# Feed-forward down products as seven block products of eight, inner features in three parts

## The chip, the cores and the metric

The kernel runs on one core of one Trainium2 chip. The metric is the device time of one execution in microseconds (us); lower is better. An execution's span runs from its first to its last instruction, and the measured time holds a little more around it.

## The reference

Two transformer blocks follow each other, on 512 tokens of 1024 features, in float32. The first has two layers, each a token mixer, a cross attention and a gated feed-forward part. The second has one layer: three token mixers (one of them `s5`, a state space model), a cross attention and a feed-forward part with a convolution over three tokens. The inner width is 2816 in all three feed-forward parts. What the change touches is this:

```python
def swiglu(h, w_gate_up, w_down):
    g, u = jnp.split(h @ w_gate_up, 2, axis=-1)
    return (jax.nn.silu(g) * u) @ w_down

def conv_ffn(h, w_up, conv_w, conv_b, w_down):
    u = h @ w_up
    u = lax.conv_general_dilated(
        u, conv_w[:, None, :], window_strides=(1,), padding=[(CONV_W - 1, 0)],
        dimension_numbers=('NWC', 'WIO', 'NWC'), feature_group_count=2 * D_FF_2) + conv_b
    gate, val = jnp.split(u, 2, axis=-1)
    return (jax.nn.silu(gate) * val) @ w_down
...
x = x + swiglu(rms_norm(x, g_ffn[i]), w_gate_up[i], w_down[i])      # i = 0, 1
x = x + conv_ffn(rms_norm_2(x, norm_ffn[l]), ffn_w_up[l], ffn_conv[l], ffn_conv_b[l], ffn_w_down[l])
```

## The kernel before, in words

Features lie on the 128 partitions and the 512 tokens along the free axis. x is eight tiles of 128x512 that stay in SBUF. Every float32 operand is kept as two float32r parts, high and low, and a product of two operands is three matmuls (`Kit.mm3`, L274 to L282: high by high, high by low, low by high) into a PSUM bank of 128x512.

Weights come from DRAM in chunks of 128x512 or 128x384 (`Kit.load_split`, L306): SP issues the DMA into a raw tile (L308), ACT casts it to the high part (L310), and the engine that `Kit.by` names subtracts the high part from the raw tile for the low part (L312; VectorE in all three feed-forward parts). There are 7 raw tiles (NRAW) and 5 of each part (NW). `Kit.split` (L246 on ACT, L243 on DVE) does the same for activations.

`First.ffn` (L1166; called with i = 0 and i = 1) and `Second.ffn` (L2342) work in two halves of the inner features. In each half 11 up steps run, one for each inner tile: `proj_g` (L315) makes the gate tile and the value tile, 24 matmuls of 512 columns each. Then they are joined: L1178 (DVE, from PSUM), L1179 (ACT, silu), L1180 (POOL) and L1183 (DVE); or in the last stage the convolution, L2351 to L2354 (one DVE product from PSUM, one ACT step, two DVE steps that add a shifted product), L2365 (ACT) and L2368 (DVE). The result is split into high and low. After the 11 up steps come eight down steps, one for each output tile of 128 features: 11 inner tiles by three matmuls of 512 columns, the weights in chunks of 512, 512 and 384, and one addition of the bank to x (L671 or L1327 on DVE). After the second half, each x tile is at once normed (`normed`, `squares` L442 on ACT and L446 on POOL) or, at the end of the program, `last` takes its squares and `finish` scales and stores it.

During `First.ffn(1)` a job of the second block is woven in: `s5_make_g`, which computes the state space model's tables from its parameters (L1816 to L2034), mostly on DVE (operations of 128x16, 128x128 and 128x144) and POOL, with PE transposes at L2029 and L1994. `Kit.fill` after each up step runs as much of it as its argument says.

The order of instructions on each engine comes out of the tile framework's scheduler, which starts from the order in which the program emits them. Each engine works through its own list in order. Scratch tiles come from `Kit.room`, with a number of tiles for each tag.

## Time and profile before

| | before |
|---|---|
| median of 3 runs | 2791.21 us (2787.19 to 2793.16) |
| span of the profiled execution | 2782.0 us |
| feed-forward up stretch, last stage, second half | 119.7 us |
| feed-forward down stretch, last stage, first half | 60.4 us |
| feed-forward down stretch, last stage, second half | 60.6 us |
| up and down of `First.ffn(1)`, first half | 144.0 and 72.1 us |

The profile is of one execution of 2782.0 us from first to last instruction. The own time of that execution is not listed beside its span; the median of the three timed runs is 9.2 us above the span. In all rows PE is TensorE, DVE is VectorE, ACT is ScalarE, POOL is GpSimd and SP is SyncE; PEld is the weight load of a matmul, which runs beside the matmul before it. In a row of a group `out<-in` gives the names of the tiles, then their shapes, the number of instructions, the busy time, the mean of one in ns, and the idle time of the engine just before with what ended it.

### The profile page before, as it was taken

Reading aid. Unit: us, or ns where it says so; the run is one execution under the profiler, and the core shown is the slowest. Engines: PE = TensorE matmul, PEld = TensorE weight load, DVE = VectorE, ACT = ScalarE, POOL = GpSimd, SP = SyncE. Lnnn points to the kernel's source line nnn. Section 1 sums busy time; section 2 is a strip of 40 time slices with the busy share of each in tenths; the row PEclk is TensorE's granted clock in tenths of the full one; section 3 lists DMA queues with packets and bytes.
Section 4 is the critical chain, followed back from the end, with each engine's and each line's share of the span. In section 5 each row is a group of like instructions: output and inputs, shape, how many; then the busy total and the mean of one; then the engine's idle time right before and its main releaser. Section 6 shows DMA issues by size and latency. Waiting matters only on the chain.

```text
span 2782.0 us, 37160 instructions
## 1 busy us (share of the span) xinstructions
PE 2675.9 (96%) x13432; PEld 2152.4 (77%) x13432; DVE 1599.8 (58%) x3076; ACT 1186.2 (43%) x2208; POOL 517.4 (19%) x439
## 2 busy tenths in 40 slices
PE   8999999999999999899999889899999999999998
PEld 6668878888776787678887777687878788888886
DVE  4676654344357967973445567535443556675673
ACT  4566543233345765332334331425223445543442
POOL 5224121011211131250112331112131300100001
PEclk8999999999999999999999989699999999999999
DMA  4112223323322131333433344312211433233332
GB/s 151 35 42 77 72 84 93 101 95 95 110 78 74 49 103 56 109 121 114 142 96 131 113 163 116 99 61 62 81 54 61 124 117 102 83 96 95 99 95 68
DMA packets 172520, 258.51 MB, mean 93 GB/s; under 512 B 42528, under 2 KB 60832, under 8 KB 172320
## 3 DMA queue, kind: packets, MB, share of 16 engines
q1 hardware_dynamic: 172336, 256.13, 29.7%
q8 instruction: 106, 1.74, 0.3%
q14 instruction: 78, 0.64, 0.1%
HBM read 234.04 MB, written 22.15 MB: 92 GB/s over the span
## 4 chain that ended last, share of the span: by engine, by line
PE 54%; DVE 6%; issue 6%; POOL 2%; ACT 1%; DMA 0%; SPq 0%; POOLq 0%; DVEq 0%; ACTq 0%
PE ps_mm L280 14%; PE ps_mm L282 14%; PE ps_mm L281 14%; PE ps_ch L591 1%; DVE wl L312 1%; PE ps_si L2128 1%; POOL rs L466 1%; PE ps_tr L620 1%; PE ps_ch L1537 1%; PE ps_si L2124 0%; PE ps_si L607 0%; PE ps_ch L1610 0%; PE ps_ch L508 0%; PE ps_ch L1611 0%; PE ps_ch L1468 0%
## 5 line engine op out<-in xcount | busy, mean ns | idle before, releaser
L310 ACT CAST wh<-wraw 128x512 fp32r<-128x512 f32 (+1 forms) x777 | 474.5, 614 | 935.4 <-PE ps_mm L281 657.1
L312 DVE TENSOR_TENSOR wl<-wraw,wh 128x512 fp32r<-128x512 f32 (+1 forms) x691 | 484.3, 704 | 359.3 <-ACT wh L310 350.1
L280 PE MATMUL ps_mm<-xs,wh 128*128 128x512 f32 x1544 | 624.2, 404 | 6.2 <-ACT wh L310 5.7
L282 PE MATMUL ps_mm<-xs,wl 128*128 128x512 f32 x1544 | 612.8, 397 | 8.2 <-DVE wl L312 6.7
L281 PE MATMUL ps_mm<-xs,wh 128*128 128x512 f32 x1544 | 614.1, 398 | 0.5 <-DVE xs L262 0.3
L280 PEld LDWEIGHTS ps_mm<-xs,wh 128*128 128x128 f32 x1544 | 293.9, 190 | 77.0 <-issue 9.1
L282 PEld LDWEIGHTS ps_mm<-xs,wl 128*128 128x128 f32 x1544 | 293.7, 190 | 75.9 <-DVE wl L312 8.5
L281 PEld LDWEIGHTS ps_mm<-xs,wh 128*128 128x128 f32 x1544 | 293.8, 190 | 63.3 <-DVE xs L262 4.5
L446 POOL TENSOR_TENSOR acc<-acc,za 128x512 f32<-128x512 f32 x59 | 82.2, 1393 | 732.1 <-ACT za L442 730.4
L280 PE MATMUL ps_mm<-za,wh 128*128 128x512 f32 x460 | 183.5, 399 | 5.6 <-ACT za L246 5.0
L282 PE MATMUL ps_mm<-za,wl 128*128 128x512 f32 x460 | 182.7, 398 | 1.3 <-DVE wl L312 1.3
L281 PE MATMUL ps_mm<-za,wh 128*128 128x512 f32 x460 | 181.3, 394 | 0.1
L312 POOL TENSOR_TENSOR wl<-wraw,wh 128x512 fp32r<-128x512 f32 x86 | 113.4, 1327 | 345.5 <-ACT wh L310 283.8
L1180 POOL TENSOR_TENSOR za<-za,za 128x512 f32<-128x512 f32 x44 | 58.3, 1325 | 508.5 <-ACT za L1179 508.5
L280 PEld LDWEIGHTS ps_mm<-za,wh 128*128 128x128 f32 x460 | 87.9, 191 | 25.0 <-ACT za L246 6.2
L282 PEld LDWEIGHTS ps_mm<-za,wl 128*128 128x128 f32 x460 | 87.8, 191 | 22.0 <-DVE wl L312 1.8
L280 PE MATMUL ps_mm<-zb,wh 128*128 128x512 f32 (+1 forms) x284 | 100.3, 353 | 4.6 <-ACT zb L246 4.1
L281 PEld LDWEIGHTS ps_mm<-za,wh 128*128 128x128 f32 x460 | 87.7, 191 | 20.7 <-DVE za L243 1.0
L281 PE MATMUL ps_mm<-zb,wh 128*128 128x512 f32 (+1 forms) x284 | 98.6, 347 | 0.0
L243 DVE TENSOR_TENSOR za<-ps_tr,za 128x512 fp32r<-128x512 f32 (+3 forms) x152 | 84.3, 558 | 24.6 <-ACT za L246 23.5
L282 PE MATMUL ps_mm<-zb,wl 128*128 128x512 f32 (+1 forms) x284 | 98.3, 346 | 0.0
L466 POOL TENSOR_TENSOR rs<-sm,neghalf 128x4 f32<-128x4 f32 (+2 forms) x32 | 44.8, 1399 | 279.4 <-DVE sm L465 273.0
(592 smaller groups left out, 5013.3 us busy)
## 6 DMA issues: line engine op xcount, KB each, us to landing
wraw<-w_gu SPq DMA_DIRECT2D x176, 256.0 KB, 2.6
wraw<-w_dn SPq DMA_DIRECT2D x96, 256.0 KB, 2.6
wraw<-w_up SPq DMA_DIRECT2D x88, 256.0 KB, 2.6
wraw<-w_gate SPq DMA_DIRECT2D x48, 256.0 KB, 2.6
wraw<-w_dn SPq DMA_DIRECT2D x48, 192.0 KB, 2.3
dram<-za SPq DMA_DIRECT2D x26, 256.0 KB, 2.2
zc<-dram SPq DMA_DIRECT2D x26, 256.0 KB, 5.0
wraw<-w_cd SPq DMA_DIRECT2D x24, 256.0 KB, 2.6
```

What stands on the lines that cost most here:

```text
L243: self.nc.vector.tensor_tensor(lo, src, hi.bitcast(F32), op=ALU.subtract)
L280: mm(out, ah, bh, start=start, stop=False, **kw)
L281: mm(out, ah, bl, start=False, stop=False, **kw)
L282: mm(out, al, bh, start=False, stop=stop, **kw)
L310: self.nc.scalar.copy(hl[0], raw)
L312: eng.tensor_tensor(hl[1], raw, hl[0].bitcast(F32), op=ALU.subtract)
L446: self.nc.gpsimd.tensor_tensor(self.acc[0], self.acc[0], sq, op=ALU.add)
L466: self.nc.gpsimd.tensor_tensor(r, ms, self.neghalf[:, :n], op=ALU.pow)
L591: self.kit.nc.tensor.matmul(p, a[:, b * 128 : b * 128 + 128], c[:, k0:k1], start=i == 0, stop=i == len(self.qk) - 1)
L620: kit.nc.tensor.transpose(tr[:, i * 128 : i * 128 + 128], self.e[b][:, c : c + n], kit.ident)
L1180: nc.gpsimd.tensor_tensor(a, a, st["rb"], op=ALU.mult)
L1537: mm(p[:, i * 256 : i * 256 + 256], blk(st["ka"], e, 2 * g + i), st["ar"][2 * g + i][rows_], start=True, stop=True)
```

## The change

The down products of all three feed-forward parts are made in blocks of 2x2: two output tiles by two inner tiles by the two halves of 256 tokens, with seven block products in place of eight. One block product of n inner pairs is 3n matmuls of 256 columns. The left factors are the weight blocks a11, a12, a21, a22 and sums of them (s1 = a21 + a22, s2 = s1 - a11, a11 - a21, a12 - s2), the right factors are halves of inner tiles and differences of them (t1 to t4).

- The inner features are three parts of 4, 4 and 3 pairs of tiles (`PARTS`), where there were two halves of 11 tiles. The weights lie in DRAM in the order that this needs.
- `forms` makes the right factors for a pair of inner tiles: four subtractions of 128x256, on POOL (on DVE for the very last pair), then one split of 128x256 and three of 128x512, where the pair had two splits of 128x512. They fill seven tiles of a new tag m.
- `blocks` loads four raw weight chunks for a pair of output tiles and a part (128x512, or 128x384 in the part of three), makes four sums of them on POOL, and splits all seven: seven casts on ACT, seven subtractions on DVE.
- `seven` makes the seven products in three banks (x, y, z), of which it uses 256 columns; `seven_added` adds the bank to a half of an x tile after each product, on DVE.
- `ffn_parts` runs the up steps one beyond the end of each part, then the four pairs of output tiles. `Kit.fill` after an up step gets 3.0 for 1.5 (and stands in the last stage too).
- There are 8 raw tiles for 7, 6 of each weight part for 5, and the rooms have other sizes. The normed x or the last squares are taken for two x tiles together.

```diff
-NRAW = 7
-NW = 5
+NRAW = 8
+NW = 6
+L, R = slice(0, S // 2), slice(S // 2, S)
+PARTS = 4, 4, 3
...
+    def forms(self, f0, f1, tiles, eng=None):
...
+        sub = (eng or nc.gpsimd).tensor_tensor
+        ta, tb = self.f(), self.f()
+        sub(ta[:, L], f0[:, R], f0[:, L], op=ALU.subtract)
+        sub(ta[:, R], f1[:, R], f0[:, R], op=ALU.subtract)
+        sub(tb[:, L], f1[:, R], ta[:, L], op=ALU.subtract)
+        sub(tb[:, R], f1[:, L], tb[:, L], op=ALU.subtract)
+        one = next(tiles)
+        out = {"b11": (one[:, L], one[:, R])}
+        self.split(f0[:, L], *out["b11"])
+        for z, a, b in ((f1, "b21", "b22"), (ta, "t1", "t3"), (tb, "t2", "t4")):
+            hl = next(tiles), next(tiles)
+            self.split(z, *hl)
+            out[a], out[b] = ([y[:, h] for y in hl] for h in (L, R))
+        return out
...
+    def blocks(self, w):
...
+        for j in range(2):
+            for h in range(2):
+                z = raw[j, h] = self.t([128, CW], "wraw", NRAW)[:, : n * 128]
+                nc.sync.dma_start(z.rearrange("p (k m) -> p k m", m=128), w[j, :, h * n : h * n + n, :])
...
+        def sum_(x, y, op):
+            z = self.f(n * 128, tag="s")
+            nc.gpsimd.tensor_tensor(z, x, y, op=op)
+            return z
...
+        yield both(a11)
+        yield both(a12)
+        s1 = sum_(a21, a22, ALU.add)
+        s2 = sum_(s1, a11, ALU.subtract)
+        yield both(s2)
+        yield both(s1)
+        yield both(sum_(a11, a21, ALU.subtract))
+        yield both(sum_(a12, s2, ALU.subtract))
+        yield both(a22)
...
+    def seven(self, w, xf, take):
...
+        def product(p, form, start):
+            hl = next(a)
+            for k, x in enumerate(xf):
+                self.mm3(p, [z[:, k * 128 : k * 128 + 128] for z in hl], x[form], start and k == 0, k == len(xf) - 1, skip_group_check=True)
...
+        x = self.bank()[:, L]
+        product(x, "b11", True)
+        take("p1", x)
+        yield us
+        y = self.bank()[:, L]
+        product(y, "b21", True)
+        take("p2", y)
+        yield us
+        product(x, "t2", False)
+        take("u2", x)
...
+        z = self.bank()[:, L]
+        product(z, "t1", True)
+        take("p5", z)
...
+        product(x, "t3", False)
+        take("u3", x)
...
+        product(z, "b22", False)
+        take("p35", z)
...
+        product(x, "t4", False)
+        take("c21", x)
...
+    def seven_added(self, w, xf, first, second):
...
+        to = dict(p1=(first, L), p2=(first, L), u2=(first, R), p5=(second, R), u3=(second, R), p35=(first, R), c21=(second, L))
+        def take(step, p):
+            z, h = to[step]
+            self.nc.vector.tensor_tensor(z[:, h], p, z[:, h], op=ALU.add)
...
+    def ffn_parts(self, up, w_dn, x, left):
...
+        for at, n in parts:
+            end = min(at + 2 * n + 1, 2 * tiles)
+            while c < end:
+                self.run(up(c, mid(c == 2 * tiles - 1)))
+                self.fill(3.0)
+                c += 1
+            i = parts.index((at, n))
+            for m in range(DT // 2):
+                self.run(self.seven_added(w_dn[i][m], pairs[at // 2 : at // 2 + n], x[2 * m], x[2 * m + 1]))
+                if i == len(parts) - 1:
+                    left(2 * m)
+                    left(2 * m + 1)
...
-                kit.run(kit.proj_g(I["w_gu"][i, half * (FT // 2) + c], xs, gate))
-                kit.fill(1.5)
-            for m in range(DT):
-                kit.run(kit.proj_g(I["w_dn"][i, half, m], mid, lambda j, p: self.down(m, p, g if half else None)))
...
+        kit.ffn_parts(up, parts_of(I["w_dn"][i]), self.x, lambda m: self.left(m, g))
...
-    kit.room("aaaa", a=50)
+    kit.room("aaaa", a=24, m=28, s=6)
...
-    kit.room("abbb", a=31, b=50-31)
+    kit.room("abbb", a=8, m=28, s=5, b=17)
```

In all, PE gets 1188 rows more (three parts with 924 matmuls of 256 columns for 528 of 512). The comments are gone, so lines have other numbers: after the change L339 is a weight chunk's low part in the up steps, L270 any low part of `split` (of weight blocks `wl` and of the factors `zm`), L360 to L363 the four subtractions of `forms`, L391 a sum of weight blocks, L447 an addition to x, L1341, L1333 and L1344 are L1178, L1180 and L1183 of before, L2130 to L2136 are L1972 to L1978, and L2509 to L2524 are L2351 to L2368. Three places show how rows move.

DVE in the down steps of `First.ffn(0)`, before: three low parts of a chunk, then an addition to x.

```order
L671 TENSOR_TENSOR x_76<-ps_ch_4819,x_76 128x512
L312 TENSOR_TENSOR wl_4916<-wraw_4913,wh_4915 128x512
L312 TENSOR_TENSOR wl_4922<-wraw_4919,wh_4921 128x384
L312 TENSOR_TENSOR wl_4963<-wraw_4960,wh_4962 128x512
L671 TENSOR_TENSOR x_90<-ps_si_4872,x_90 128x512
```

The same place after the change.

```order
L270 TENSOR_TENSOR wl_4831<-wraw_4822,wh_4830 128x512
L447 TENSOR_TENSOR x_76<-ps_mm_4683,x_76 128x256
L270 TENSOR_TENSOR wl_4849<-wraw_4824,wh_4848 128x512
L447 TENSOR_TENSOR x_90<-ps_si_4748,x_90 128x256
L270 TENSOR_TENSOR wl_4870<-zs_4867,wh_4869 128x512
L447 TENSOR_TENSOR x_90<-ps_mm_4683,x_90 128x256
```

A low part and an addition now take turns; the low part is of a product six further on, of a raw block or of a sum `zs`. POOL had no row in the down steps.

POOL in the same down steps after the change: the four sums of each group of seven products, with work of a later inner tile and pair between.

```order
L391 TENSOR_TENSOR zs_4727<-wraw_4688,wraw_4690 128x512
L391 TENSOR_TENSOR zs_4729<-zs_4727,wraw_4684 128x512
L391 TENSOR_TENSOR zs_4766<-wraw_4684,wraw_4688 128x512
L391 TENSOR_TENSOR zs_4785<-wraw_4686,zs_4729 128x512
L360 TENSOR_TENSOR za_4583<-za_4462 128x256
L391 TENSOR_TENSOR zs_4865<-wraw_4826,wraw_4828 128x512
L1333 TENSOR_TENSOR za_4541<-za_4541,za_3919 128x512
L391 TENSOR_TENSOR zs_4867<-zs_4865,wraw_4822 128x512
L361 TENSOR_TENSOR za_4583<-za_4541,za_4462 128x256
```

What moved here is new work on an engine that had none in this place, with two inputs in SBUF in each row.

DVE in `First.ffn(1)`, the last block of the woven job before the change, beside the eleventh up step (L1183 joins it, L243 splits it).

```order
L1978 SCALAR_TENSOR_TENSOR zb_12116<-zb_12116,zb_12129 128x144
L1183 TENSOR_TENSOR za_12043<-ps_mm_12059,za_12043 128x512
L1974 TENSOR_TENSOR zb_12115<-zb_12115,zb_12117 128x144
L1972 TENSOR_TENSOR zb_12115<-zb_11375,zb_11226 128x144
L1973 TENSOR_TENSOR zb_12117<-zb_11375,zb_11226 128x144
L1978 SCALAR_TENSOR_TENSOR zb_12116<-zb_12116,zb_12136 128x144
L243 TENSOR_TENSOR za_12086<-za_12043,za_12085 128x512
```

The end of the same block after the change, beside the eighth up step.

```order
L2130 TENSOR_TENSOR zb_12658<-zb_12085,zb_11940 128x144
L2131 TENSOR_TENSOR zb_12660<-zb_12085,zb_11940 128x144
L1341 TENSOR_TENSOR za_12830<-ps_mm_12805,za_11577 128x512
L2132 TENSOR_TENSOR zb_12658<-zb_12658,zb_12660 128x144
L2136 SCALAR_TENSOR_TENSOR zb_12659<-zb_12659,zb_12665 128x144
L339 TENSOR_TENSOR wl_12984<-wraw_12981,wh_12983 128x512
L270 TENSOR_TENSOR wl_13042<-wraw_13033,wh_13041 128x512
L1344 TENSOR_TENSOR za_12830<-ps_mm_12846,za_12830 128x512
```

The whole job now lies ahead of the ninth up step. Before the gate row L1341 of this excerpt, 62 rows of the job stand in a line without a row of the feed-forward part between them; before the change the block's 64 rows were spread from the tenth up step into the first down steps.

## Rows read from the trace of the kernel before

**Rows 1.** The page: busy time of each engine, and the chain that ended last by engine.

```profile
PE 2675.9 (96%) x13432; PEld 2152.4 (77%) x13432; DVE 1599.8 (58%) x3076; ACT 1186.2 (43%) x2208; POOL 517.4 (19%) x439
...
PE 54%; DVE 6%; issue 6%; POOL 2%; ACT 1%; DMA 0%; SPq 0%; POOLq 0%; DVEq 0%; ACTq 0%
```

**Rows 2.** Busy time by stretch: us, engines' busy us (instructions), granted clock, DMA share, GB/s.

```profile
1094.90:1238.90 144.00, 128.79 (x582) 106.12 (x581) 119.73 (x410) 53.40 (x91) 52.10 (x72) 0.95 0.36 116
1238.90:1311.00 72.10, 68.28 (x318) 53.98 (x317) 32.80 (x70) 14.86 (x26) 13.22 (x16) 0.93 0.35 110
1434.10:1494.60 60.50, 60.50 (x267) 49.63 (x265) 27.26 (x40) 27.72 (x47) 17.39 (x12) 1.00 0.32 99
1168.80:1180.65 11.85, 0.43 (x2) 0.04 (x2) 11.74 (x27) 2.28 (x4) 8.88 (x14) 0.62 0.31 107
2526.00:2586.40 60.40, 60.40 (x266) 49.54 (x265) 23.22 (x36) 15.60 (x27) 0.00 (x0) 1.00 0.32 98
2586.40:2706.10 119.70, 119.70 (x530) 99.07 (x529) 87.98 (x128) 57.69 (x87) 0.00 (x0) 1.00 0.31 96
2706.10:2766.70 60.60, 60.60 (x267) 49.73 (x265) 20.55 (x32) 22.62 (x36) 7.80 (x6) 1.00 0.19 55
```

**Rows 3.** Groups by line in the last stage's first down stretch, 2526.0 to 2586.4 us.

```profile
L282 PEld LDWEIGHTS ps_mm<-za,wl 128*128 128x128 f32 x88 | 16.5, 188 | 3.9
L312 DVE TENSOR_TENSOR wl<-wraw,wh 128x512 fp32r<-128x512 f32 x17 | 11.7, 687 | 18.0 <-ACT wh L310 18.0
L310 ACT CAST wh<-wraw 128x512 fp32r<-128x512 f32 x18 | 11.2, 623 | 30.9 <-PE ps_mm L281 30.9
...
L312 DVE TENSOR_TENSOR wl<-wraw,wh 128x384 fp32r<-128x384 f32 x7 | 3.9, 559 | 10.7 <-ACT wh L310 10.7
```

**Rows 4.** Timeline of PE, 995.95 to 1003.99 us: start, duration, instruction.

```profile
995.95 0.28 PE L281 MATMUL ps_mm<-zb,wh 128*128 128x256 f32 x1
...
998.54 0.28 PE L282 MATMUL ps_mm<-zb,wl 128*128 128x256 f32 x1
...
998.89 0.28 PE L282 MATMUL ps_mm<-wh,zb 128*128 128x256 f32 x1
...
1003.99 0.28 PE L282 MATMUL ps_mm<-wh,zb 128*128 128x256 f32 x1
```

**Rows 5.** Timeline at 283 us and at 1120.7 us: POOL and DVE side by side.

```profile
283.00 1.77 POOL L446 TENSOR_TENSOR acc<-acc,za 128x512 f32<-128x512 f32 x1
283.53 0.68 DVE L671 TENSOR_TENSOR x<-ps_mm,x 128x512 f32<-128x512 f32 x1
...
284.13 1.19 DVE L312 TENSOR_TENSOR wl<-wraw,wh 128x512 fp32r<-128x512 f32 x1
...
1120.68 0.18 DVE L1872 TENSOR_TENSOR zb<-zb 128x16 f32<-128x16 f32 x1
1120.74 1.29 POOL L1180 TENSOR_TENSOR za<-za,za 128x512 f32<-128x512 f32 x1 [6.89 <-ACT za L1179]
...
1120.89 1.17 DVE L1874 TENSOR_TENSOR zb<-zb 128x16 f32<-128x16 f32 x1
```

**Rows 6.** Waits, 1094.9 to 1240 us: engine, line, waited for: us, times, longest.

```profile
PE ps_ch L2029 <- DVE zb L2022: 11.4, 1, 11.4
```

**Rows 7.** Timeline of DVE: the gates of the first and the ninth up tile.

```profile
1109.56 0.69 DVE L1178 TENSOR_TENSOR za<-ps_mm,za 128x512 f32<-128x512 f32 x1 [1.37 <-ACT za L501]
...
1210.98 0.69 DVE L1178 TENSOR_TENSOR za<-ps_mm,za 128x512 f32<-128x512 f32 x1 [0.34 <-PE ps_mm L282]
```

**Rows 8.** Groups by line of small operations: DVE 1100 to 1260, POOL 1094.9, DVE 880, DVE 2586.4.

```profile
L1972 DVE TENSOR_TENSOR zb<-zb,zb 128x144 f32<-128x144 f32 x16 | 6.2, 388 | 0.0
...
L1949 POOL TENSOR_TENSOR zb<-zb,zb 128x256 f32<-128x256 f32 x1 | 0.9, 885 | 0.0
...
L1083 DVE TENSOR_TENSOR zb<-ps_mm,zb 128x256 f32<-128x256 f32 x4 | 1.7, 421 | 0.3 <-PE ps_mm L282 0.3
...
L2354 DVE SCALAR_TENSOR_TENSOR za<-za,vecs,za 128x511 f32<-128x511 f32 x21 | 15.8, 751 | 6.1 <-ACT za L2352 6.1
```

More of the change, by code (lines that the diff above doesn't have):

```diff
@@ L51, in tiled, with halved, parted, parts_of @@
     return c.reshape(-1, n, *c.shape[1:])
+def halved(w):
+    t = w.reshape(w.shape[0] // 128, 128, -1)
+    return np.concatenate([t[0::2], t[1::2]]).reshape(w.shape)
+def parted(w):
+    out, at = [], 0
+    for n in PARTS:
+        out.append(tiled(halved(w[at * 256 : (at + n) * 256])).reshape(-1))
+        at += n
+    return np.concatenate(out)
+def parts_of(src):
+    out, at = [], 0
+    for n in PARTS:
+        size = D * n * 256
+        out.append(src[at : at + size].rearrange("(c j p k m) -> c j p k m", j=2, p=128, k=2 * n, m=128))
+        at += size
+    return out
 def col(v):
@@ L327, in proj_late @@
+    def seven_added(self, w, xf, first, second):
[3 more added lines that the diff above has]
+            self.nc.vector.tensor_tensor(z[:, h], p, z[:, h], op=ALU.add)
+        return self.seven(w, xf, take)
     def proj_late(self, groups, last):
@@ L423, in flush, with mid, f @@
             self.fill(1.0)
+    def ffn_parts(self, up, w_dn, x, left):
+        parts, tiles, mids = [], sum(PARTS), []
+        for n in PARTS:
+            parts.append((2 * sum(PARTS[: len(parts)]), n))
+        pairs = []
+        held = (self.f(S, F32R, tag="m") for _ in range(7 * tiles))
+        def mid(last):
+            def f(z):
+                mids.append(z)
+                if len(mids) % 2 == 0:
+                    pairs.append(self.forms(*mids[-2:], held, self.nc.vector if last else None))
+            return f
+        c = 0
+        for at, n in parts:
[10 more added lines that the diff above has]
+                    left(2 * m + 1)
     def normed(self, m, x, g, squares=True):
@@ L1157, in cross, with left, ffn @@
                       lambda: kit.ended(O, 3))
-    def down(self, m, p, g):
+    def left(self, m, g):
         if callable(g):
-            self.add(m, p)
             g(m)
         else:
-            self.add(m, p, g)
-    def ffn(self, i, g=None):
+            self.kit.normed(m, self.x[m], g[:, m : m + 1])
+    def ffn(self, i, g):
         kit, nc, I = self.kit, self.nc, self.I
@@ L2355, in conv, with up, emit @@
             return a
[L2357 to L2380 removed]
+        def up(c, mid):
+            def emit(j, p):
+                if "rb" not in st:
+                    st["rb"] = kit.spread(kit.rstd(), 4)
+                a = conv(p, j * FT + c)
+                if j == 0:
+                    nc.scalar.activation(a, a, AF.Silu)
+                    st["a"] = a
+                else:
+                    nc.vector.tensor_tensor(a, a, st["a"], op=ALU.mult)
+                    mid(a)
+            return kit.proj_g(I["w_up2"][c], xs, emit)
+        for m in range(DT):
+            if self.x[m] is None:
+                raise ValueError(m)
+        kit.ffn_parts(up, parts_of(I["w_dn2"]), self.x, self.last)
     def last(self, m):
@@ L2468, in program @@
     s.cross()
-    kit.room("aaaa", a=50)
+    kit.room("aaaa", a=24, m=28, s=6)
     s.ffn()
```

90 lines of the change are left out of this document (42 added, 48 removed).

## The prediction

> **What bounds the kernel now.** I read the page first. PE is busy 96% of the span, VectorE (DVE) 58%, ScalarE (ACT) 43% and POOL 19%, and on the chain that ended last PE has 54% and DVE 6% [rows 1]. So a down stretch should be as long as its matmuls. The stretches show that it is: in the last stage's first down stretch PE is busy 60.40 of 60.40 us at granted clock 1.00 (2.4 GHz), DVE 23.22 us, POOL not at all; the second is 60.6 us [rows 2]. The two halves, 121.0 us, hold 528 matmuls of 512 columns, .229 us each. Their weight parts are made far ahead: ACT's casts wait for PE to give tiles back (30.9 us of idle) and DVE's low parts for ACT (18.0 us) [rows 3]. Fewer columns on PE are worth their time here, as long as DVE and POOL can take what replaces them.
>
> The first half of the second feed-forward part is different. There the woven job keeps DVE busy 119.73 of 144.00 us, PE stands at 128.79, and the granted clock is 0.95; the down stretch behind it takes 72.10 us [rows 2]. The undisturbed pair is 119.7 and 60.4 [rows 2], so 36 us go to the job. One wait, of transposes for DVE, is 11.4 us [rows 6], and in that stretch the clock falls to 0.62, between 1.2 and 2.4 GHz, after PE stood with 0.43 us of work in 11.85 [rows 2].
>
> **The change, part by part.**
>
> *Fewer columns.* The trace has no down product of 256 columns, but the same form elsewhere, each matmul with its own weight load: 22 starts from 995.95 to 998.54, .1177 us each, with a scratch tile moving and a weight chunk standing as after the change; and 45 from 998.89 to 1003.99, .1133 us, with the roles exchanged [rows 4]. I take .1177, whose operands are those of the change. 924 x .1177 = 108.8 us per part against 121.0: **-12.2**. The other end, .1133, gives 104.7: -16.3.
>
> *The seven splits and additions of a group.* A group of seven products is 84 matmuls (n = 4; 9.89 us) or 63 (n = 3; 7.42 us); there are eight of the first and four of the second. ACT's seven casts, .623 us each [rows 3], make 4.4 us: hidden. DVE has seven low parts at .687 and seven additions of 128x256 from PSUM at .421 [rows 3, 8]: 7.8 us, below 9.89 (n = 3, with .559 for .687: 6.9 below 7.42). New are POOL's four sums, 1.29 us each, and here a price hides. While POOL works on two SBUF tiles, a DVE operation whose inputs are both in SBUF is held: a 128x16 operation took 1.17 us where its neighbour took 0.18, and a low part 1.19 where .687 is usual [rows 3, 5]. An addition from PSUM beside the same POOL operation took 0.68, unharmed [rows 5]. POOL's row began at 1120.74 and the held one, short itself, ended at 1122.06, so a sum holds the port some 1.15 us. Sums and low parts then need 4 x 1.15 + 7 x .687 = 9.4 us of 9.89; with n = 3 and three quarters of 1.15, 3.45 + 3.91 = 7.4 of 7.42. It just fits if the additions lie beside the sums. Order gives them turns [low part, addition], so part of each sum will meet a low part. I add 0.1 us a group, **+1.2** per part. The bounds are nothing, and all the additions left over, 2.95 us in each group (below).
>
> The Trainium skill ("SBUF — State Buffer", section "SBUF: two separate sides") calls the pair of ports that DVE and GpSimd share an exclusive lock: whichever starts first has it for its whole instruction and the other fully blocks, and for DVE this concerns instructions with two SBUF inputs. The trace agrees in kind, with a hold of about 1.15 of POOL's 1.29 us; by the rule's whole 1.29 the sum of a group is 4 x 1.29 + 7 x .687 = 10.0 us, an estimate, which would make the group DVE's by 0.1 us.
>
> *The up steps.* `forms` adds 1.5 low parts a pair, 1.04 us of DVE, and four POOL subtractions at .885 [rows 8] or less. In the last stage DVE is busy 87.98 of 119.70 us and POOL idle [rows 2]: 11 x 1.04 us over 22 up steps fit. The cover is the rest of DVE, some 30 us. Cost: nothing. The steps run in parts of 9, 8 and 5, so that PE has an up step while a pair's factors are made; not for the last pair. There the factors wait for subtractions and splits after the last up tile, on DVE: some 3 x .421 + 3 x .687 = 3.3 us, against the two or so us that the scheduler covers with products of the earlier pairs. **+1** in the two parts of the first block. In the last stage the convolution's chain stands ahead, with two steps at .751 [rows 8] and the casts between: **+2.3**.
>
> *Ends.* Two x tiles, not one, are normed together: +.5, and +.8 at the end of the program, where their squares come before the last sum. SP issues four weight loads a group for six; DMA is at .19 to .36 [rows 2]: nothing. Other rooms and two more buffers move rows elsewhere; between -5 and +5, and I take -1.
>
> *The job.* It is now done by the ninth up step. Up to that gate the rows after the change, each at the mean of its line between 1090 and 1440 us in the trace, make 118.7 us of DVE where the same sum over the order before is 104.6; the trace took 101.4 for that stretch, 1109.56 to 1210.98 [rows 7], and scaled by that the new order takes 115.1. So the ninth gate comes 13.7 us later, in two places: ahead of the first transposes (factors of three pairs are in front of them), and in the last block, 64 rows at up to .388 [rows 8] with PE idle. Behind it nothing of the job is left, and of the 36 us above those that came after 1210.98 vanish: from there to the end of the part's last down stretch, 1494.6 [rows 2], it was 283.6 us; a clean run of 13.5 up steps at 10.88 and 121.0 us is 267.9, so 15.7. The balance is -2. The clock may take some back after a long wait, so I take **+2**, with -5 and +12 as ends.
>
> *The sum.* First part: -12.2 + 1.2 + 1 + .5 = -9.5. Last part: -12.2 + 1.2 + 2.3 + .8 = -7.9. Second part: -12.2 + 1.2 + 1 + .5 + 2 = -7.5. With -1 elsewhere: -25.9. The profiled execution spans 2782.0 us, so 2756.1; the median of the runs lies 9.2 above the span, so **2765** on the clock of the runs (2791.21 - 25.9). Its own range, 2757 to 2778, comes from half of the ends above.
>
> **The rivals.**
>
> *Fully fed.* The additions fall beside the sums, nothing is late, and a matmul takes between .1133 and .1177. For it: DVE is busy a third of the down stretch now [rows 2]. Against: the fit above has 0.5 us to spare. Three parts at -12.2 to -16.3, ends as above or none: 2742 to 2757, say 2750.
>
> *The shared port bounds the down steps* (the other side). A low part and an addition alternate in DVE's queue, so a held low part also holds the addition behind it, PE's next product on that bank waits, and ACT's next cast waits for PE. What part of the 2.95 us of additions isn't covered decides: half of it makes groups of 9.4 + 1.5 = 10.9 and 7.4 + 1.5 = 8.9, 122.8 us a part, slower than 121.0; the break-even is a little less than half. With +1.8 a part and +7 for the ends and the job: 2791.2 + 5.4 + 7 = 2804. All of it: 8 x 12.35 + 4 x 10.35 = 140 us, 2855. For it: the rows at 284 and 1120 us. Against: the addition from PSUM passes [rows 5].
>
> *The job eats its part's gain.* DVE is saturated in nine up steps, waits grow past 12 us, and the clock stays at 1.2 GHz for longer. Second part: -12.2 + 2.7 + 17 = +7.5 with the other two as summed: 2780.
>
> *Half the columns don't halve the time.* If the weight load bound it, at .188 each [rows 3], 924 would take 174 us and the three parts +158: 2950. The 67 matmuls of rows 4 speak against it.
>
> **How the numbers follow.** My forecast has .46, fully fed .26, the job .13, the port .13, the weight load .02. The range reaches from the lower end of fully fed, 2742, to 2798, which takes in the job's case and leaves out most of the port's. A measurement of this kernel tells 0.2% (5.6 us) from no change. Faster by more than that: the first three, less their upper tails, .80; within it: .07; slower: the port but its low end, and the weight load, .13.
>
> **What would show it.** In the changed profile's down stretches of the last stage: PE's matmuls .1177 apart, a part's three stretches together near 110 us, POOL at 4 to 5 us a group. Right on the port if low parts of the down steps average some .8 to 1.0 us while additions stay at .42. Wrong if PE waits there for low parts or additions by over a microsecond a group, if the wait for the job's first transposes is over 20 us, or if the last pair's factors cost over 4 us.

## The result, and the profile after

The changed kernel takes 2830.48 us (median of 4 runs, 2824.72 to 2831.86) against 2792.18 before (4 runs). The ratio is 1.0139, 95% interval [1.0121, 1.0156]: 1.4% slower, where I had forecast 0.9% faster. The profiled execution spans 2827.8 us, 45.8 more than before.

The page first; its columns are those of [rows 1].

```profile
PE 2674.0 (95%) x14620; PEld 2197.1 (78%) x14620; DVE 1892.4 (67%) x3466; ACT 1266.2 (45%) x2384; POOL 839.9 (30%) x703
...
PE 51%; DVE 10%; issue 4%; POOL 2%; ACT 2%; DMA 0%; POOLq 0%; DVEq 0%; SPq 0%; ACTq 0%
```

DVE is busy 293 us longer and POOL 323 (a row that is held counts as busy while it is held); DVE's part of the chain that ended last rose from 6 to 10%. The next view is busy time by stretch of the changed kernel (columns as in [rows 2]): the three feed-forward parts whole; then the three down stretches of `First.ffn(0)`; the first nine up steps of `First.ffn(1)` and its three down stretches; the three down stretches of the last stage.

```profile
366.10:737.10 371.00, 359.80 (x2005) 313.36 (x2004) 247.35 (x364) 152.54 (x261) 150.52 (x122) 0.99 0.31 94
1103.70:1531.20 427.50, 387.28 (x2161) 327.55 (x2162) 332.69 (x721) 167.54 (x293) 202.18 (x197) 0.95 0.35 105
2435.00:2812.40 377.40, 359.75 (x2001) 315.25 (x1999) 316.90 (x457) 179.06 (x295) 117.80 (x96) 0.98 0.28 84
...
471.40:512.50 41.10, 40.15 (x337) 39.75 (x337) 35.53 (x57) 17.71 (x29) 13.39 (x11) 1.00 0.34 99
599.60:641.40 41.80, 40.17 (x337) 39.81 (x336) 36.22 (x57) 17.70 (x29) 13.20 (x11) 1.00 0.33 98
695.80:737.10 41.30, 33.96 (x258) 31.18 (x258) 38.96 (x66) 23.01 (x44) 17.96 (x15) 1.00 0.28 85
1103.70:1261.10 157.40, 131.67 (x612) 99.62 (x613) 142.22 (x437) 53.77 (x95) 85.86 (x107) 0.88 0.33 103
1261.10:1304.30 43.20, 40.27 (x338) 39.86 (x337) 37.43 (x60) 17.32 (x30) 19.11 (x13) 1.00 0.57 175
1391.30:1432.70 41.40, 39.36 (x338) 38.80 (x338) 36.96 (x57) 17.71 (x29) 14.61 (x12) 1.00 0.35 104
1487.10:1531.20 44.10, 34.58 (x254) 32.14 (x253) 42.19 (x66) 27.01 (x52) 24.59 (x19) 0.96 0.26 79
2535.90:2583.00 47.10, 42.18 (x338) 41.76 (x338) 42.34 (x66) 21.20 (x35) 15.15 (x12) 0.93 0.32 92
2670.10:2716.90 46.80, 41.65 (x337) 41.24 (x336) 42.42 (x65) 21.17 (x35) 14.69 (x11) 0.96 0.30 91
2771.30:2812.40 41.10, 34.11 (x253) 31.86 (x252) 35.61 (x65) 21.75 (x42) 16.30 (x14) 0.96 0.07 20
```

Before, the three parts took 368.3, 399.7 and 363.6 us (from the run of matmuls that begins the first up step to the last matmul of the down steps), so they changed by +2.7, +27.8 and +13.8 us. The rest, +1.5, lies in stages that the change hardly touches. Of down stretches, four pairs should be 336 matmuls x .1177 = 39.5 us and three 29.7. None is: PE is busy in 34.0 to 42.2 us of stretches of 41.1 to 47.1, and DVE in 36 to 42 of each of the nine. (In the third line of `First.ffn(0)`'s stretches, .9 us of the 41.3 are four matmuls of the next stage.)

The matmuls are as forecast. Timeline of PE in the changed kernel: 51 starts, .1178 us each.

```profile
2551.09 0.28 PE L309 MATMUL ps_mm<-zm,wl 128*128 128x256 f32 x1
...
2557.10 0.28 PE L309 MATMUL ps_mm<-zm,wl 128*128 128x256 f32 x1
```

DVE is not. Groups by line on DVE in the first down stretch of `First.ffn(0)`, columns as in [rows 3].

```profile
L270 DVE TENSOR_TENSOR wl<-zs,wh 128x512 fp32r<-128x512 f32 x13 | 12.3, 949 | 0.8 <-ACT wh L273 0.5
L270 DVE TENSOR_TENSOR wl<-wraw,wh 128x512 fp32r<-128x512 f32 x10 | 9.5, 946 | 0.2
L447 DVE TENSOR_TENSOR x<-ps_mm,x 128x256 f32<-128x256 f32 x15 | 6.3, 418 | 1.4 <-PE ps_mm L309 1.1
```

A low part takes .95 us on average where it took .687 before [rows 3], and an addition from PSUM keeps its .42 [rows 8]. The timeline of POOL and DVE shows why.

```profile
2550.24 1.30 POOL L391 TENSOR_TENSOR zs<-wraw,wraw 128x512 f32<-128x512 f32 x1 [5.45 <-DVE wl L270]
...
2550.35 0.42 DVE L447 TENSOR_TENSOR x<-ps_mm,x 128x256 f32<-128x256 f32 x1 [0.19 <-PE ps_mm L309]
...
2552.22 1.30 POOL L391 TENSOR_TENSOR zs<-wraw,zs 128x512 f32<-128x512 f32 x1 [0.68 <-POOL zs L391]
...
2552.34 1.72 DVE L270 TENSOR_TENSOR wl<-zs,wh 128x512 fp32r<-128x512 f32 x1
```

The addition at 2550.35 runs beside the sum; the low part at 2552.34 waits for it, 1.72 us for a work of .687. In the last stage this happens at the start of the stretch too, where the convolution of the up step that runs ahead is on DVE; its shifted products have two SBUF inputs. Timeline of DVE and POOL there:

```profile
2538.47 2.40 DVE L2512 SCALAR_TENSOR_TENSOR za<-za,vecs,za 128x511 f32<-128x511 f32 x2
2538.63 1.70 POOL L391 TENSOR_TENSOR zs<-wraw,zs 128x512 f32<-128x512 f32 x1 [1.23 <-DVE wl L270]
...
2543.30 0.41 DVE L447 TENSOR_TENSOR x<-ps_mm,x 128x256 f32<-128x256 f32 x1
```

The two convolution steps take 2.40 us where 2 x .751 [rows 8] is 1.5; the row at 2543.30 is the first addition of the stretch. Waits of the changed kernel, 2535.9 to 2583.0 us, then 1103.7 to 1261.1 us (columns as in [rows 6]).

```profile
PE ps_mm L307 <- DVE x L447: 4.8, 1, 4.8
```

```profile
PE ps_ch L2187 <- DVE zb L2180: 17.4, 3, 9.1
PE ps_mm L307 <- DVE za L1341: 3.2, 1, 3.2
```

PE waits 4.8 us for the first addition, which stands behind held operations in DVE's list: seven held rows of DVE between 2526.5 us and the addition (low parts, splits and convolution steps) took some 4.9 us more than such rows take unheld, .68 or .75 us for each operation (an estimate from that timeline). Most of the rest of the stretch's excess of 7.6 us is a lower clock behind the wait: PE was busy 42.18 us with what is 39.5 at 2.4 GHz, and from 2541 to 2546 us the granted clock was 0.55, between 1.2 and 2.4 GHz. The job's transposes wait 17.4 us, in three pieces, where before they had 11.4 [rows 6].

### The profile page after: what moved, and what is told of

It reads as the page before. It is cut to its first block, busy times and chain, and to the rows that moved or that the text cites. A ratio compares the mean times of both kernels' runs of the same rounds, so it can differ in the third digit from the quotient of the medians.

```text
span 2827.8 us, 40698 instructions
## 1 busy us (share of the span) xinstructions
PE 2674.0 (95%) x14620; PEld 2197.1 (78%) x14620; DVE 1892.4 (67%) x3466; ACT 1266.2 (45%) x2384; POOL 839.9 (30%) x703
## 4 chain that ended last, share of the span: by engine, by line
PE 51%; DVE 10%; issue 4%; POOL 2%; ACT 2%; DMA 0%; POOLq 0%; DVEq 0%; SPq 0%; ACTq 0%
PE ps_mm L307 13%; PE ps_mm L308 13%; PE ps_mm L309 13%; PE ps_ch L746 1%; DVE wl L270 1%; DVE wl L339 1%; DVE za L2512 1%; PE ps_si L2286 1%; POOL rs L621 1%; PE ps_tr L775 1%; PE ps_ch L613 1%; PE ps_ch L1695 1%; PE ps_ch L1626 0%; DVE x L447 0%; PE ps_ch L1768 0%
## 5 line engine op out<-in xcount | busy, mean ns | idle before, releaser
L307 PE MATMUL ps_mm<-xs,wh 128*128 128x512 f32 (+1 forms) x1536 | 626.1, 408 | 10.6 <-ACT wh L337 5.8
L308 PE MATMUL ps_mm<-xs,wh 128*128 128x512 f32 (+1 forms) x1536 | 616.2, 401 | 5.3 <-DVE xs L289 5.0
L309 PE MATMUL ps_mm<-xs,wl 128*128 128x512 f32 (+1 forms) x1536 | 614.5, 400 | 2.1 <-POOL wl L339 1.5
L339 DVE TENSOR_TENSOR wl<-wraw,wh 128x512 fp32r<-128x512 f32 x547 | 402.3, 739 | 169.8 <-ACT wh L337 164.3
L307 PEld LDWEIGHTS ps_mm<-xs,wh 128*128 128x128 f32 (+1 forms) x1536 | 294.7, 192 | 84.1 <-issue 14.8
L308 PEld LDWEIGHTS ps_mm<-xs,wh 128*128 128x128 f32 (+1 forms) x1536 | 295.2, 192 | 70.7 <-DVE xs L289 10.4
L309 PEld LDWEIGHTS ps_mm<-xs,wl 128*128 128x128 f32 (+1 forms) x1536 | 294.8, 192 | 68.7 <-issue 3.3
L307 PE MATMUL ps_mm<-zm,wh 128*128 128x256 f32 x724 | 207.9, 288 | 29.8 <-DVE x L447 24.0
L308 PE MATMUL ps_mm<-zm,wh 128*128 128x256 f32 x724 | 205.6, 284 | 2.4 <-DVE zm L270 2.4
L339 POOL TENSOR_TENSOR wl<-wraw,wh 128x512 fp32r<-128x512 f32 x86 | 113.3, 1326 | 313.7 <-ACT wh L337 282.7
L309 PE MATMUL ps_mm<-zm,wl 128*128 128x256 f32 x724 | 205.1, 284 | 0.9 <-DVE wl L270 0.9
L307 PEld LDWEIGHTS ps_mm<-zm,wh 128*128 128x128 f32 x724 | 138.6, 192 | 35.8 <-DVE x L447 11.0
L308 PEld LDWEIGHTS ps_mm<-zm,wh 128*128 128x128 f32 x724 | 139.2, 192 | 3.7 <-DVE zm L270 3.4
L270 DVE TENSOR_TENSOR wl<-zs,wh 128x512 fp32r<-128x512 f32 (+1 forms) x144 | 134.2, 937 | 10.8 <-ACT wh L273 8.1
L309 PEld LDWEIGHTS ps_mm<-zm,wl 128*128 128x128 f32 x724 | 139.2, 192 | 1.1 <-DVE wl L270 1.1
L270 DVE TENSOR_TENSOR zm<-za,zm 128x512 fp32r<-128x512 f32 (+1 forms) x132 | 113.9, 863 | 38.2 <-ACT zm L273 32.9
L391 POOL TENSOR_TENSOR zs<-wraw,wraw 128x512 f32<-128x512 f32 (+1 forms) x72 | 93.5, 1298 | 138.1 <-DVE wl L270 70.6
L1333 POOL TENSOR_TENSOR za<-za,za 128x512 f32<-128x512 f32 x44 | 58.8, 1337 | 228.7 <-ACT za L1332 228.5
```

Source lines behind the costliest of these rows:

```text
L270: self.nc.vector.tensor_tensor(lo, src, hi.bitcast(F32), op=ALU.subtract)
L307: mm(out, ah, bh, start=start, stop=False, **kw)
L308: mm(out, ah, bl, start=False, stop=False, **kw)
L309: mm(out, al, bh, start=False, stop=stop, **kw)
L339: eng.tensor_tensor(hl[1], raw, hl[0].bitcast(F32), op=ALU.subtract)
L391: nc.gpsimd.tensor_tensor(z, x, y, op=op)
```

## The experiments

Theory A is that the shared port makes the loss: POOL's operations and DVE's with two SBUF inputs exclude each other. Theory B is that DVE simply has too much to do. C to G concern single places.

**The sums elsewhere, and gone.**

```diff
 # e1
-            nc.gpsimd.tensor_tensor(z, x, y, op=op)
+            nc.vector.tensor_tensor(z, x, y, op=op)
 # e2
-            z = self.f(n * 128, tag="s")
-            nc.gpsimd.tensor_tensor(z, x, y, op=op)
-            return z
+            return x
```

> The changed kernel (2830.5 us) with the four sums of weight blocks of each group on DVE in place of POOL. Theory A, the shared port: the low parts of the down steps last 0.82 to 0.95 us because POOL's sums hold them, so without POOL in the way they fall to 0.69, the four-pair down stretches of First.ffn(0) go from 41.1 and 41.8 us to 39.5 to 40.5, and the whole to 2810 to 2825 us. Theory B, DVE's load alone: four operations of 0.69 more in each group lengthen DVE's list from 7.8 to 10.5 us against 9.9 of PE, down stretches grow by 2 to 4 us each and the whole goes to 2840 to 2860 us.

> The changed kernel with the sums of weight blocks left out (the split takes the first operand of each sum as it is, so the products are of other weights); all else is as in the changed kernel. Theory A, the shared port: low parts at 0.69 us, four-pair down stretches at 39.5 to 40, the three-pair ones at 33 to 35 for 36 to 44, the whole 15 to 25 us below the changed kernel. Theory B, DVE's load alone: low parts keep 0.69 once POOL is out, but PE goes on waiting for additions, less than 8 us in all.

e1 took 2821.1 us, ratio 1.0102 [1.0060, 1.0143] to the kernel before. That interval overlaps the changed kernel's, so the stretches decide. DVE has more work and the stretch is shorter: 40.2 us in the first down stretch of `First.ffn(0)` for 41.1, and low parts are at .689, as theory A said. (The nine up steps of `First.ffn(1)` are not shorter, 160.6 us for 157.4.) Groups by line on DVE there, in e1:

```profile
L270 DVE TENSOR_TENSOR wl<-zs,wh 128x512 fp32r<-128x512 f32 x13 | 9.0, 689 | 0.7
L270 DVE TENSOR_TENSOR wl<-wraw,wh 128x512 fp32r<-128x512 f32 x10 | 6.9, 687 | 0.7 <-ACT wh L273 0.2
```

Theory B's lengthening did not come in `First.ffn(0)`. e2, which leaves the sums out, took 2789.8 us in a single execution, 40 below the changed kernel, more than either theory said. Stretches of e2: the first four-pair one, the last one of `First.ffn(0)`, and the first nine up steps of `First.ffn(1)`.

```profile
468.30:507.90 39.60, 39.60 (x338) 39.60 (x337) 31.72 (x57) 17.71 (x29) 1.12 (x1) 1.00 0.37 122
689.00:726.40 37.40, 33.71 (x258) 31.12 (x257) 34.61 (x66) 22.67 (x44) 10.50 (x7) 1.00 0.35 105
1093.30:1247.20 153.90, 130.78 (x611) 98.61 (x612) 136.46 (x437) 53.51 (x95) 79.17 (x102) 0.89 0.31 103
```

Without sums the first four-pair stretch is PE's 39.6 (40.3 in the last stage). The last stretch keeps 7.7 us above 29.7 and the job's stretch hardly moves, so the sums are not what makes these two long.

**The factors on DVE, alone and with the sums.**

```diff
 # e6, e12 (with e1's edit)
-        sub = (eng or nc.gpsimd).tensor_tensor
+        sub = nc.vector.tensor_tensor
```

> The changed kernel (2830.5 us) with the four subtractions of every pair's factors on DVE, as for the last pair, in place of POOL. Theory A, the shared port: on POOL they take up to 1.1 us each (40 rows, 43.6 us in First.ffn(1)) and hold the low parts and the job's operations, on DVE 0.42 each; the first nine up steps of First.ffn(1) go from 157.4 to 145 to 152 us and the whole falls by 5 to 15 us. Rival: they lie in slack or DVE has none, and the whole stays within 4 us.

> The changed kernel with both the sums of weight blocks and the subtractions of the factors on DVE, so that the change brings no work to POOL. Theory A, the shared port: no low part of the down steps is held any more, and what the two single moves gave (9 and 12 us, one of them from one look) adds up in part: 2808 to 2818 us. Theory B, DVE's load: DVE is then over 95% busy in every down stretch and the whole stays at 2818 us or above, far from the 2790 us that the kernel without the sums took.

> The kernel of e12 again, for its profile. Theory A: low parts and factors' splits at 0.69 us throughout, POOL with nothing but the gates, norms and the job in the feed-forward parts; against the changed kernel the first nine up steps of First.ffn(1) fall from 157.4 to 140 to 148 us, and the down stretches of the last stage from 47.0, 46.8 and 40.4 to 42 to 44, 42 to 44 and 36 to 38. Theory B: DVE is busy over 95% in every down stretch and First.ffn(0) gains nothing over the run with the sums on DVE.

e6 took 2818.5 us in a single execution, a fall of the size forecast but not in the place: the nine up steps stayed at 158.1 us. The stage of the mixers between the second and the last part, which has no edit, was 895 us there against 904; that is most of the 12. Its first down stretch of `First.ffn(0)` says more. Busy time of that stretch in e6, and a low part of its DVE:

```profile
466.10:505.60 39.50, 39.00 (x338) 38.81 (x337) 35.24 (x57) 17.71 (x29) 10.19 (x8) 1.00 0.32 102
...
L270 DVE TENSOR_TENSOR wl<-zs,wh 128x512 fp32r<-128x512 f32 x13 | 12.2, 940 | 1.2 <-ACT wh L273 0.9
```

The sums are on POOL and hold the low parts, .94 us on average, as in the changed kernel, and yet the stretch is 39.5 us. So four sums a group do fit there (the second stretch is 40.6); what does not fit is the sums together with what else POOL does beside them.

e12 took 2795.0 us, ratio 1.0025 [1.0007, 1.0043], better than theory A's 2808 to 2818 and far from B's: the same operations on DVE in place of POOL take back 35 of the 38 us. Stretches of e12b (the same kernel, a single execution of 2801.3 us): parts; then the first four-pair stretch and the last stretch of `First.ffn(0)`; the nine up steps and the last stretch of `First.ffn(1)`; the three stretches of the last stage.

```profile
363.60:726.00 362.40, 357.36 (x2001) 312.33 (x2000) 254.05 (x451) 153.06 (x260) 45.45 (x34) 0.99 0.31 95
1095.50:1517.30 421.80, 388.57 (x2163) 329.46 (x2164) 332.38 (x810) 166.75 (x292) 99.32 (x109) 0.95 0.34 107
2425.90:2784.20 358.30, 354.31 (x2001) 310.96 (x1999) 307.45 (x545) 181.07 (x294) 8.82 (x7) 1.00 0.29 89
...
469.00:508.60 39.60, 39.60 (x338) 39.59 (x337) 34.60 (x64) 17.70 (x29) 0.00 (x0) 1.00 0.35 103
689.70:726.00 36.30, 32.54 (x254) 30.52 (x253) 35.34 (x72) 22.01 (x43) 8.84 (x7) 1.00 0.26 84
1095.50:1245.80 150.30, 127.64 (x611) 96.36 (x612) 134.76 (x455) 50.90 (x90) 64.35 (x85) 0.90 0.32 106
1470.60:1517.30 46.70, 38.67 (x256) 36.20 (x255) 42.39 (x75) 26.38 (x51) 15.58 (x10) 0.85 0.24 74
2526.90:2566.40 39.50, 39.50 (x337) 39.50 (x336) 36.50 (x70) 18.94 (x31) 0.00 (x0) 1.00 0.35 103
2653.50:2693.10 39.60, 39.60 (x337) 39.57 (x336) 36.60 (x70) 19.04 (x31) 0.00 (x0) 1.00 0.33 101
2747.60:2784.20 36.60, 33.19 (x253) 31.46 (x251) 32.55 (x69) 21.05 (x40) 6.57 (x5) 0.95 0.08 22
```

With POOL out of it, DVE is busy 34.6 to 36.6 us of these four-pair stretches, and PE is never late: 39.5 us, the 336 matmuls and nothing else. The same DVE with less work of its own had cost 1.6 to 7.6 us a stretch when POOL worked beside it. (In `First.ffn(1)` the second four-pair stretch is 39.5 us too; the first, right behind the job, is 43.4.) Against the changed kernel the three parts gain 8.6, 5.7 and 19.1 us. Against its expectation the last stage did better (39.5 and 39.6 us for 42 to 44) and the nine up steps worse (150.3 for 140 to 148).

In the last stage neither move alone did that (its first stretch is 43.6 us in e1, 46.5 in e6). In e6 POOL's sums still hold the convolution's steps, up to 1.75 us for .75, and PE waits 4.0 us for the first addition. In e1 POOL's three subtractions just ahead of the stretch hold a sum and a split (1.11 and 1.23 us for .68), which is some 1.0 of the 2.3 us that PE waits; whether the order of DVE's list makes the rest is open.

The excess of the last stretches, 36.3, 46.7 and 36.6 us for 29.7, stays, and the middle one is longer than in the changed kernel (44.1). In the first block DVE is busy 35.3 of 36.3 and 42.4 of 46.7 us there, so theory B's load is the likely limit. In the last stage it is busy 32.6 of 36.6, less than in a four-pair stretch that had no late matmul; there PE's longest wait is 2.2 us, for the last pair's factors.

**The order of the parts and the step ahead.**

```diff
 # e4
-            end = min(at + 2 * n + 1, 2 * tiles)
+            end = min(at + 2 * n, 2 * tiles)
 # e7
-PARTS = 4, 4, 3
+PARTS = 3, 4, 4
```

> The changed kernel without the one up step past the end of each of the first two parts. Theory E: in the last stage that step's convolution chain stands on DVE ahead of the first products' low parts and additions and costs the waits of 4.8 and 4.6 us at the start of the down stretches (and some 2 us of lower clock behind each); without it the waits go, but the last pair's factors then come late, 3 to 6 us a stretch, so the whole is within 6 us of the changed kernel. Rival: the step is a plain loss, and the whole falls by 10 us or more.

> The changed kernel with the part of three pairs first and parts of four behind (3, 4, 4 for 4, 4, 3). Theory F: the last down stretches (36.3, 44.0 and 40.4 us where 252 matmuls at 0.1177 make 29.7) are long because the norm's or the last squares' work on DVE and POOL, which before had 60.5 us of down steps to lie beside, now has four groups of 7.4 us; beside groups of 9.9 us the last stretches take 41 to 46 us against 39.5, and the whole falls by 6 to 12 us. Rival: the excess is a cost for each group and comes along, the whole stays within 3 us.

e4 took 2854.4 us in a single execution, 24 above the changed kernel: both sides of the expectation missed. The step ahead is worth more than its wait: without it the first two down stretches of `First.ffn(0)` are 43.6 and 45.6 us for 41.1 and 41.8, and the first of the last stage 48.8 for 47.1. e7 took 2845.7 us, ratio 1.0202 [1.0180, 1.0223], 15 above the changed kernel; theory F fell, and its rival's 3 us were too few. (The expectation's 36.3 us for the first last stretch is 41.3 up to its last matmul.) Last stretches of e7's three parts:

```profile
693.10:740.80 47.70, 41.77 (x338) 40.08 (x336) 42.73 (x66) 26.28 (x45) 21.74 (x16) 1.00 0.26 84
1498.30:1549.10 50.80, 41.61 (x337) 39.79 (x336) 48.54 (x68) 29.43 (x51) 29.39 (x20) 1.00 0.25 83
2784.70:2834.40 49.70, 42.84 (x337) 41.31 (x335) 42.43 (x65) 24.87 (x44) 20.80 (x14) 0.97 0.09 28
```

The excess over PE's 39.5 us, 8 to 11 us, came along with a part of four, so more matmuls do not cover it.

**The woven job.**

```diff
 # e3 (changed kernel)
-                self.fill(3.0)
+                self.fill(1.5)
 # e10 (kernel before)
-                kit.fill(1.5)
+                kit.fill(3.0)
```

> The changed kernel with the woven job handed out as before (1.5 for 3.0 after each up step). Theory C, the job's crowding: First.ffn(1) took 427.5 us against 399.7 before because DVE and POOL get the whole job within eight up steps; spread again, its first nine up steps go from 157.5 to 120 to 130 us, some 8 us come back in the down steps behind, and the whole is 12 to 22 us below the changed kernel. Theory D, DVE's total in this part binds wherever the job lies: the part stays at 422 to 428 us, the whole within 5 us.

> The kernel before the change, with nothing changed but the woven job handed out twice as fast (3.0 for 1.5 after each up step of First.ffn). Theory C, crowding: the job within fewer up steps costs by itself, since its DVE and POOL operations then stand back to back and hold each other and PE starves; First.ffn(1) goes from 399.7 to 410 to 425 us and the whole to 2800 to 2815 us. Theory D, DVE's total: without the factors and the additional low parts and additions the same order costs little, First.ffn(1) stays within 5 us of 399.7 and the whole at 2786 to 2797 us.

> The changed kernel with First.ffn(1), the part with the woven job, as before the change (halves of 11, its room of before, 1.5 after each up step); the other two parts stay changed, sums on POOL. Theory C: that part alone accounts for 28 of the 39 us, so the whole is 2799 to 2806 us. Rival: its loss was mostly that of neighbours or of the buffers, and the whole stays above 2815 us.

e9 took 2802.0 us, ratio 1.0040 [1.0019, 1.0061]: `First.ffn(1)` alone accounts for 28 of the 39 us, as said. e3 took 2834.9 us, ratio 1.0155 [1.0121, 1.0189]: handing the job out more slowly in the changed kernel gains nothing (the nine up steps fall to 130.9 us, the down stretches rise to 51.0 and 48.9, and the part is 434.9 us). That is against theory C and near theory D. e10 took 2799.0 us, ratio 1.0031 [1.0015, 1.0047]: in the kernel before, the faster job costs some 9 us, with the part at 407.8 for 399.7, between what the two theories said.

The rows of the job on DVE tell crowding and port apart. Its 358 operations take 97.7 us before, 103.2 in e10 (crowded, nothing new on POOL), 103.2 in e12b (crowded, the change's work on DVE) and 112.9 in the changed kernel (sums of their rows). So crowding lengthens them by 5.5 us and POOL's new work by another 9.7. The 27.8 us themselves don't split as cleanly: e10 shows 8.1 for crowding in the kernel before, e12b wins back only 5.7, and its part is still 22.1 us longer than before. DVE is busy 332.4 us in that part of e12b and 228.7 in e9, where the part is as before; that this load makes the rest is argued and not shown.

**Versions.** e8 has seven products in `First.ffn(0)` alone, sums on DVE. e13 is e12 with `First.ffn(1)` as before. e11 and e14 take seven products for the first two parts of `First.ffn(0)` and the middle part of `First.ffn(1)`, plain products of 512 columns for the other parts of these two and the last stage as before; e11 has the sums on DVE, e14 the factors too. e15 is e14 with seven products in the first two parts of the last stage. All of e11, e14 and e15 hand the job out as before, and keep the step ahead.

```diff
 # e15
+KINDS = (7, 7, 8), (8, 7, 8), (7, 7, 8)
...
+            if kinds[i] == 7:
+                for m in range(DT // 2):
+                    self.run(self.seven_added(w_dn[i][m], [plain[q] for q in range(at // 2, at // 2 + n)], x[2 * m], x[2 * m + 1]))
...
+            else:
+                for m in range(DT):
...
+                    self.run(self.proj_g(w_dn[i][m], [done[q] for q in range(at, at + 2 * n)], emit))
```

> Seven products in First.ffn(0) alone, with the sums on DVE; First.ffn(1) and the last stage as before the change, in their rooms of before (8 raw tiles and 6 of each part stay). Theory A and the run with sums on DVE: First.ffn(0) takes 361 us for 368.3 and the other two return to 399.7 and 363.6, so the whole is 2781 to 2788 us, 0.1 to 0.4% below the kernel before. Rival: the deeper buffers or the other rooms cost time elsewhere by themselves, and the whole is at 2795 us or above.

> The kernel of e12 with First.ffn(1) as before the change (halves of 11, its room of before, 1.5 after each up step): seven products in First.ffn(0) and the last stage, sums and factors on DVE. Theory C (what is left is the part with the job): First.ffn(1) returns to 399.7, the other two take 358 to 362 and 360 to 366 us for 368.3 and 363.6, the whole 2775 to 2786 us. Rival: First.ffn(1) had gained as well once the port was free, and the whole stays at 2790 us or above.

> Seven products only where DVE has room: the first two parts of First.ffn(0) and the middle part of First.ffn(1), with the sums on DVE; the last parts and the part beside the woven job as plain products of 512 columns in the same three parts; the last stage as before the change; 1.5 after each up step. If DVE's load is the limit that the other runs show, First.ffn(0) takes 355 to 360 us (40.1 and 40.1 for the four-pair stretches as in the run with sums on DVE, 33 to 34 for the plain one) for 368.3, First.ffn(1) 394 to 402 for 399.7, and the whole is 2774 to 2786 us, below both kernels. Rival: the factors' work shows up elsewhere and the whole is at 2788 us or above.

> The kernel of e11 with the factors' subtractions on DVE too. Theory A: their 0.42 us on DVE cost less than the holds by POOL, First.ffn(0) and (1) lose 1 to 3 us each, the whole 2774 to 2783 us and below the kernel before by 0.2 to 0.5%. Rival: nothing is held in these parts any more, and the whole is within 3 us of e11's 2783.

> The kernel of e14 with seven products also in the first two parts of the last stage (sums and factors on DVE), plain products in its last part. Theory G, DVE's load beside the last squares and norms: a part of three pairs costs 33.0 us as 144 plain matmuls of 512 columns against 36.3 us as 252 of 256 in the run with all on DVE; the last stage's down stretches take 39.5, 39.5 and 33 us, the stage 354 to 357 for 363.6, and the whole is 2768 to 2776 us, 0.5 to 0.9% below the kernel before. Rival: the last stretch takes 36 us as plain products too, because what is late there is the last up tile, and the whole stays at 2776 us or above.

| | us | ratio to before, 95% interval |
|---|---|---|
| e8 | 2788.4 | 0.9990 [0.9970, 1.0010] |
| e11 | 2783.2 | 0.9987 [0.9970, 1.0004] |
| e13 | 2784.0 | 0.9985 [0.9974, 0.9996] |
| e14 | 2779.7 | 0.9965 [0.9948, 0.9983] |
| e15 | 2768.7 | 0.9943 [0.9922, 0.9964] |

e8 and e11 can't be told from the kernel before, e13 barely. e14 and e15 are faster than both kernels. e8 came out .4 us above its range, with `First.ffn(0)` at 363.6 us for 361; the four others lie in theirs. Two details missed: `First.ffn(1)` took 405.8 us in e11 for 394 to 402, and e14 against e11 is longer in `First.ffn(0)` (359.0 for 357.4) and shorter in `First.ffn(1)` (399.3), not shorter in both. Stretches of e15: the three parts, then the last stage's three down stretches.

```profile
366.50:725.30 358.80, 357.52 (x1892) 308.69 (x1891) 227.59 (x387) 147.45 (x244) 46.92 (x35) 0.99 0.32 99
...
1092.70:1494.10 401.40, 378.26 (x1909) 315.93 (x1908) 267.53 (x675) 150.90 (x255) 100.06 (x111) 0.97 0.36 114
...
2397.00:2751.60 354.60, 354.02 (x1892) 306.18 (x1891) 281.52 (x478) 175.23 (x277) 10.05 (x8) 1.00 0.29 90
2498.00:2537.50 39.50, 39.50 (x337) 39.48 (x336) 36.52 (x70) 18.99 (x31) 0.00 (x0) 1.00 0.33 103
2624.70:2664.20 39.50, 39.50 (x337) 39.50 (x336) 36.70 (x70) 19.20 (x31) 0.00 (x0) 1.00 0.33 102
2718.50:2751.60 33.10, 33.10 (x145) 26.86 (x144) 13.82 (x23) 16.27 (x27) 7.79 (x6) 1.00 0.08 23
```

Theory G's times hold: a last stretch of three pairs is 33.1 us as plain products and 36.6 as seven, though seven have fewer columns. Each of the three stretches is now PE's own time. Plain products take both away, DVE's load (13.8 us for 32.6) and the last pair's factors, so this run does not say which of the two counted.

## Why the prediction was wrong

The miss is 71.7 us of span, -25.9 forecast and +45.8 measured: 12.2 of it in `First.ffn(0)` (-9.5 and +2.7), 35.3 in `First.ffn(1)` (-7.5 and +27.8), 21.7 in the last stage (-7.9 and +13.8), 2.5 elsewhere. The last stage's three down stretches were to be near 110 us together; they are 135.0, where the two of before took 121.0.

*Fewer columns*: right. .1178 us each, and 39.5 us for a four-pair stretch once PE is fed.

*The seven splits and additions*: this step failed first. It had the right mechanism and even the right hold, and found that sums and low parts need 9.4 of 9.89 us, which "just fits", at +0.1 us a group. For the four sums alone that was right in `First.ffn(0)`: e6, with only the sums on POOL, has a stretch of 39.5 us there. Two things were wrong. The port has more users than the four sums: the factors' subtractions on POOL and, in the last stage, the convolution's shifted products on DVE were booked with the up steps, at "Cost: nothing", though the scheduler runs them inside and just ahead of the down stretch. And a fit of totals is no fit in time: DVE's list is in order, so a held row delays the addition behind it, the bank, and PE. Measured excess: 1.6 and 2.3 us a stretch in `First.ffn(0)` (.4 and .6 a group for +0.1), 3.7 and 1.9 in `First.ffn(1)`, 7.6 and 7.3 in the last stage, there with the lower clock behind the wait; e12b brings the first and the last part's to 0.1 or less.

*Ends and the last part*: this failed as well. I priced the last pair's factors and the ends at 1.5 to 3.1 us, and port and DVE as in any three-pair group. The factors' price was about right: PE waits 1.1 us for them in `First.ffn(0)` (+1 forecast) and 2.7 in the last stage (+2.3), with a granted clock of 0.83 behind it from 2777 to 2787 us. In the first block I left out that the last down steps hold the norms' low parts (six rows of DVE in that stretch of `First.ffn(0)`, 1.29 us each in the changed kernel and .74 in e12b), which before lay beside 60.5 us of matmuls where DVE was busy 27 [rows 2]; PE's longest waits there are for additions, 5.3 us in all. The last stage has no such rows on DVE. Excess over 29.7: 11.6 (with .9 of the next stage), 14.4 and 11.4 us. e12b leaves 6.6, 17.0 and 6.9 of it, so most of it isn't the change's work on POOL; e15's plain products take it away.

*The job*: +2 with ends at -5 and +12 was far off; the part lost 27.8 us where -7.5 was forecast. The timeline of DVE in the changed kernel has the gates that answer to [rows 7]:

```profile
1121.33 0.69 DVE L1341 TENSOR_TENSOR za<-ps_mm,za 128x512 f32<-128x512 f32 x1 [2.61 <-ACT za L656]
...
1256.21 0.68 DVE L1341 TENSOR_TENSOR za<-ps_mm,za 128x512 f32<-128x512 f32 x1
```

The ninth gate comes 134.9 us after the first, not 115.1. I had priced the rows at their means in the old order, but these depend on what POOL does beside them: the job's rows took 97.7 us before and 112.9 after, 9.7 of the 15.2 through the change's work on POOL. And DVE is not the only one to wait: the transposes stand between up steps in PE's list, so PE waits where DVE is late (17.4 us of waits for 11.4). The part's down stretches are even shorter than before (128.7 us for 132.6), so the whole loss lies in its up steps, +31.7; how much of that is DVE's load stays open.

*Elsewhere*: -1 was forecast, +1.5 measured. The stage of the mixers alone differs by 9 us between e6 and the changed kernel, which are alike there, so nothing is explained.

*The rivals.* The shared port, at .13, came, and so did the job's rival, also at .13: the second part lost 27.8 us where that rival said 7.5. The measured time lies between the port's 2804 and 2855, but that is in part luck: the port's price has +7 us for the ends and the job together, and of the 44.3 us that the three parts lost, the down stretches that it is about make 13.4 (387.9 us for 374.5 before) and the up steps of `First.ffn(1)` 31.7.

## What to carry to other kernels

Work that is moved to an idle engine isn't free when that engine shares a port with the busy one: here, giving POOL's new work to the fuller DVE made the kernel 1.1% faster (ratio 1.0139 to 1.0025). Before a saving on PE is booked, list everything that the other engines do in that stretch, work of other stages that the scheduler puts there included, and follow the in-order list behind its longest hold instead of comparing sums. A transformation that trades PE time for DVE work can be applied stretch by stretch, only where DVE has room (e15, .6% below the kernel before).
